# Background turns one projection unit later in the dense stages of a two-layer decoder trunk

## The chip, the cores and the metric

The kernel runs on one core of a Trainium2 chip. Its time is device microseconds (us) from launch to end, the median of several executions; 1670.02 us before (three executions, 1669.08 to 1671.56). All times below are in us unless marked ns.

## The reference

256 tokens of width 2048 go through two layers. Layer 0 is a projection into twelve groups of 512 columns (retention q, k, v, gate, and two halves of a convolution branch), retention over two chunks of 128 for four heads, beside it a gated 31-tap convolution with a layer norm, and an output projection. Layer 1 is a sparse attention: a projection to 16 query heads, 4 key and value heads and a small indexer (16 heads of 64, one key of 64, 16 weights), the 64 best keys of each query by the indexer's score, softmax attention over those, an output projection. After each of the two a residual layer norm and a mixture of experts follow: a router picks 2 of 16 experts, each with a gate-and-up projection (2048 to 1024) and a down projection (512 to 2048), and a second residual layer norm.

```python
m = retention_conv_mixer(h, ...) if layer % 2 == 0 else dsa_mixer(h, ...)
h = layer_norm(DEEPNORM_ALPHA * h + m, mix_ln_g[layer], mix_ln_b[layer])
f = grouped_moe(h, router_w, router_b, moe_w_gu[layer], moe_w_down[layer])
h = layer_norm(DEEPNORM_ALPHA * h + f, ffn_ln_g[layer], ffn_ln_b[layer])
```

## The kernel before

**Stages.** The program is one stream: dense stage of layer 0 (span 0 to about 395), experts of layer 0 (to about 857), dense stage of layer 1 (to about 1195), experts of layer 1 (to the end). Weights come in chunks of 1 MB through SyncE's DMA queue into pages of on-chip memory. At most `ringmax` chunks are held: 4 or 5 in the dense stages, 11 from the point `close_act` on, 20 and then fewer in the experts. A chunk is requested as soon as a page is free.

**Units.** A dense stage is cut into units. A unit is 256 rows of one 512-column weight group: ScalarE copies the piece to a rounded high part, VectorE or GpSimd subtracts for the low part (`split`, L243 and L246, the two engines by turns), and TensorE does 12 matmuls (`mm`, L284 to L286). Eight units make a group. The split of a unit is issued three units ahead of its matmuls. In layer 0 units 0 to 95 are the input projection and 96 to 127 the output projection; the output projection begins with the convolution half of its operand, so units 96 to 99 use that and the retention half is first used by unit 100. In layer 1 units 0 to 15 are the indexer's queries (two groups), 16 to 19 its key and weights (`kiwi_done`, one narrow group), 20 to 27 k, 28 to 35 v, 36 to 67 the four groups q0 to q3 of four heads each, and from 68 on the output projection.

**Order.** Each engine works through its own queue in the order in which the program issues. For unit u the order is: splits of unit u+3, matmuls of u, then, if u is the last of its group, the group's `done` (for q, k and the indexer a rotation: 8 VectorE operations on the accumulator, L703 to L706, and 4 GpSimd additions, L707 and L708), then the hooks of u, and then one step of background work (`bg(1.3)`).

**Background tasks.** Smaller work is written as generators in a queue of tasks. `yield c` with c above 0 charges c to the budget of 1.3 of this step; `yield -1` puts the task aside until the step behind the next unit. So every `yield -1` moves all that follows in that task one unit on. The tasks that the change touches are:

- `conv_ln` of layer 0: normalizes the convolution (`cn`, L548, on VectorE), waits, transposes it on TensorE (`psd`, L556), applies Silu on ScalarE and splits it. Retention heads are other tasks in the same queue.
- `ret_T` of layer 0, a hook: turns a quarter of the gated retention (`sgt`, made at `start_out`, L653) on TensorE (`psr`, L663), and splits it for the output projection. The last one is followed by `close_act`, which opens the ring to 11.
- `kiwi_done.task` of layer 1: turns the indexer's key and weights (`pki`), rotates them, turns the key again (`pki2`, which the trace shows as `pki` L1284), and goes on to the index scores and the top-64 mask.
- `turn` of layer 1: waits, then turns a rotated group on TensorE (`psq`, L1297). It is called once for each of the two indexer query groups, for k, and for each of the four q groups. For a q group the task goes on behind the turn to its four heads, each in four steps that follow one unit after the other: score (`psl` on TensorE, the scaled maximum `amx` with its negation L1395 on VectorE, the exponent L1397 on ScalarE), scaling (reciprocal L1399 and two scalings of `p`, L1401, on VectorE), transposition (`psp`, L1405, TensorE, and a copy to `pT`), output (`pso`, L1411 to L1413, and a copy to `oT`). Heads start one unit apart.

In front of unit 68 `start_out` runs tasks without a budget until 12 heads are finished, and then splits those heads' output for the output projection (`ohi` on ScalarE L1423, `olo` on VectorE L1424):

```python
def start_out():
    while held["heads"] < 12:
        self.bg(1e9)
    self.drop(4)
    oo["hi"], oo["lo"] = self.halves("ohi"), self.halves("olo")
    halves(range(0, 12, 2))
```

Of the kernel before, what the change touches and what calls it, by code (L numbers as in the profile page):

```python
# [80 lines left out]
class Trunk:  # L81
# [376 lines left out]
    def even(self):  # L458
# [6 lines left out]
        def xprep(kp):  # L465
            def f():
                ps = self.psum("psx").rearrange("p (k n) -> p k n", k=2)
                for j in range(2):
                    for t in range(2):
                        c = (2 * kp + j) * P  # L470
                        nc.tensor.transpose(ps[:, j, t * P:(t + 1) * P], self.acc[t][:, c:c + P], self.ident)
                s = slice(2 * kp % 8, 2 * kp % 8 + 2)
                hi, lo = xhi[kp // 4][:, s, :], xlo[kp // 4][:, s, :]
                nc.scalar.activation(hi, ps, AF.Copy)
                nc.vector.tensor_tensor(lo, ps, hi.bitcast(F32), ALU.subtract)
            return f
# [23 lines left out]
        def conv(j, u):  # L500
            if j == 0:
                pg["up"], pg["cy"] = self.page("up", [P, 8, S]), self.page("cy", [P, 8, S])
            up, cy = pg["up"], pg["cy"]
            yield -1
            yield -1
            for b2 in range(2):
                ps = self.psum("psu").rearrange("p (k n) -> p k n", k=2)
                for b in range(2):
                    for t in range(2):
                        c = (b2 * 2 + b) * P  # L510
                        nc.tensor.transpose(ps[:, b, t * P:(t + 1) * P], u[:, t, c:c + P], self.ident)
                c = j * 4 + b2 * 2
                nc.scalar.activation(up[:, c:c + 2, :], ps, AF.Copy)
            yield -1
            for c0 in (j * 4, j * 4 + 2):
                ps = self.psum("pcv").rearrange("p (c n) -> p c n", c=2)
                for i in range(TAPS):
                    for c in (c0, c0 + 1):
                        y, w = ps[:, c - c0, i:], self.cw[:, c, TAPS - 1 - i:TAPS - i]
                        if i:  # L520
                            nc.vector.scalar_tensor_tensor(y, up[:, c, 0:S - i], w, y, op0=ALU.mult, op1=ALU.add)  # L521
                        else:
                            nc.vector.tensor_scalar(y, up[:, c, :], w, self.cvec[:, c:c + 1], op0=ALU.mult, op1=ALU.add)
                        yield 0.33
                nc.scalar.activation(cy[:, c0:c0 + 2, :], ps, AF.Copy)
            if j == 1:
                yield from conv_ln()

        def conv_ln():
            cy = pg["cy"]  # L530
            cn = self.page("cn", [P, 2, 1024])
            self.drop()
            st = ap.tile([P, 2, 2, 6], F32, name="cst6")
            mv = ap.tile([P, 2, 2], F32, name="cmv")
            rs = ap.tile([P, 2], F32, name="crs")
            for t in range(2):
                for h in range(2):
                    ps = self.psum("psc")
                    for b in range(4):
                        nc.tensor.transpose(ps[:, b * P:(b + 1) * P], cy[:, h * 4 + b, t * P:(t + 1) * P], self.ident)  # L540
                    nc.vector.bn_stats(st[:, t, h, :], ps)
                    nc.scalar.activation(cn[:, t, h * 512:(h + 1) * 512], ps, AF.Copy)
                    yield 0.6
                nc.vector.bn_aggr(mv[:, t, :], st[:, t].rearrange("p a b -> p (a b)"))
            self.rstd(rs, mv[:, :, 1])
            yield -1
            for t in range(2):
                nc.vector.tensor_scalar(cn[:, t, :], cn[:, t, :], mv[:, t, 0:1], rs[:, t:t + 1], op0=ALU.subtract, op1=ALU.mult)  # L548
                yield 0.6
            yield -1  # L550
            for kp in range(4):
                ps = self.psum("psd").rearrange("p (k n) -> p k n", k=2)
                for b in range(2):
                    for t in range(2):
                        c = (kp * 2 + b) * P
                        nc.tensor.transpose(ps[:, b, t * P:(t + 1) * P], cn[:, t, c:c + P], self.ident)  # L556
                for b in range(2):
                    c = kp * 2 + b
                    nc.scalar.activation(cy[:, c, :], ps[:, b, :], AF.Silu, bias=self.cvec[:, 16 + c:17 + c], scale=self.cvec[:, 8 + c:9 + c])
                yield 0.3  # L560
            self.drop()
            hi, lo = cc["c"] = [self.page(f"cc{n}c", [P, 8, S], F32R) for n in ("hi", "lo")]
            for c in range(0, 8, 2):
                nc.scalar.activation(hi[:, c:c + 2, :], cy[:, c:c + 2, :], AF.Copy)
                nc.vector.tensor_tensor(lo[:, c:c + 2, :], cy[:, c:c + 2, :], hi[:, c:c + 2, :].bitcast(F32), ALU.subtract)
                yield 0.6
            self.drop()
# [88 lines left out]
        def ret_T(j, b2):  # L656
            def f():
                sg = held["g", j]
                ps = self.psum("psr").rearrange("p (k n) -> p k n", k=2)
                for b in range(2):  # L660
                    for t in range(2):
                        c = (b2 * 2 + b) * P
                        nc.tensor.transpose(ps[:, b, t * P:(t + 1) * P], sg[:, t, c:c + P], self.ident)  # L663
                k = j * 4 + b2 * 2
                hi, lo = cc["hi"][0][:, k:k + 2, :], cc["lo"][0][:, k:k + 2, :]
                nc.scalar.activation(hi, ps, AF.Copy)
                nc.vector.tensor_tensor(lo, ps, hi.bitcast(F32), ALU.subtract)
            return f
# [6 lines left out]
        n = 12 * 8  # L675

        def close_act():
# [2 lines left out]
            self.tasks.append(self.router(0))  # L680
            self.rings(11)
            self.table(AF.Sigmoid)
        hooks = {("pre", n): [start_out], n + 0: [ret_T(0, 0)], n + 1: [ret_T(0, 1)], n + 2: [ret_T(1, 0)],
                 n + 3: [ret_T(1, 1), close_act], ("pre", 0): [xprep(0)], ("split", 0): [xprep(1), lambda: self.warm(3)], ("pre", 1): [xprep(2), xprep(3)]}
        for i in range(2, 6):
            hooks["pre", i] = [xprep(i + 2)]
        self.dense(self.units(gin) + self.units(gout, self.eorder), self.moe_begin, hooks)
# [521 lines left out]
    def odd(self):  # L1209
# [57 lines left out]
        def kiwi_done(ac):  # L1267
            kw = kw80
            nc.scalar.activation(kw, ac[0][:80, 0:S], AF.Copy)

            def task():
                yield -1
                ps = self.psum("pki").rearrange("p (t n) -> p t n", t=4)
                for t in range(2):
                    nc.tensor.transpose(ps[:, t, 0:80], kw[:, t * P:(t + 1) * P], self.ident[:80, :80])
                for t in range(2):
                    self.rope(k2[:, t, 0, :], ps[:, t, 0:64], icos[:, t, :], isin[:, t, :], 1, 32)
                V.tensor_scalar(wi, ps[:, 0:2, 64:80], 1.0 / 32.0, None, op0=ALU.mult)
                nc.gpsimd.tensor_copy(k2[:, :, 1, :], k2[:, :, 0, :])
                yield 1.0  # L1280
                yield -1
                ps = self.psum("pki2")
                for t in range(2):
                    nc.tensor.transpose(ps[:, t * P:(t + 1) * P], k2[:, t].rearrange("p a b -> p (a b)"), self.ident)  # L1284
                nc.scalar.activation(kiT, ps[:, 0:S], AF.Copy)
                yield from index()
            self.tasks.append(task())

        def turn(r, dst, c0):
            yield -1  # L1290
            yield -1
            for b2 in range(2):
                ps = self.psum("psq").rearrange("p (k n) -> p k n", k=2)
                for b in range(2):
                    for t in range(2):
                        c = (b2 * 2 + b) * P
                        nc.tensor.transpose(ps[:, b, t * P:(t + 1) * P], r[:, t, c:c + P], self.ident)  # L1297
                nc.scalar.activation(dst[:, c0 + b2 * 2:c0 + b2 * 2 + 2, :], ps, AF.Copy)
# [43 lines left out]
        def k_done(ac):  # L1342
            r = t4("kr")
            for t in range(2):
                self.rope(r[:, t, :], ac[t], cos[:, t, :], sin[:, t, :], 4, 64)
            self.tasks.appendleft(turn(r, kT(), 0))
# [102 lines left out]
        n = 4 + 8 * 8  # L1449
        hooks = {("pre", n): [start_out], ("pre", n + 12): [last_heads, close_act]}  # L1450
# [103 lines left out]
```

## Time and profile before

| what | us |
|---|---|
| median of three executions | 1670.02 |
| profiled execution | 1669.06 |
| its span, first to last instruction | 1667.3 |
| TensorE busy, summed over the execution | 1629.0 |
| mean granted TensorE clock, share of full | 0.992 |

TensorE is drawn busy for all but some 38 us of the span. Ends of matmuls are modelled in the trace, so a matmul is drawn longer than the distance to the next one; a stall is read from the distance between two starts. The window view gives, per stretch, the busy time of each engine, the granted clock of TensorE and the busy share of the DMA engines.

### The profile page before, as it was taken

The page shows a single profiled execution, that of the slowest core. Times are in us where ns is not written, and L with a number is a line of the kernel's source. Part 1 is how long each engine was busy: PE and PEld are TensorE (multiplying, and loading weights), DVE is VectorE, ACT ScalarE, POOL GpSimd, SP SyncE. Part 2 cuts the span into 40 slices and gives each one's busy share as a digit, 9 for nine tenths or more (in the row PEclk, how much of TensorE's full clock was granted, in tenths as well). Part 3 has the DMA queues.
Part 4 walks back from the last instruction along what each step waited for, and adds up shares of the span by engine and source line. Part 5 has one row for each costly group of instructions (what it writes and reads, how often), then busy time and mean ns, then how long its engine had stood idle before and what let it go on. Part 6 is the DMA issues. An engine that isn't in the chain of part 4 may idle for free. (4 is left out here: it accounts for less than half of the span.)

```text
span 1667.3 us, 21366 instructions
## 1 busy us (share of the span) xinstructions
PE 1629.0 (98%) x8449; PEld 1019.7 (61%) x8449; DVE 783.9 (47%) x1467; ACT 529.0 (32%) x852; POOL 361.4 (22%) x247
## 2 busy tenths in 40 slices
PE   9999999998999999999999999999899999999998
PEld 7888887786435443544357788878635444454534
DVE  5699987633133232335245585664313222322624
ACT  5334345433211211121135444554312221212112
POOL 2446564541000000010004544344200000001001
PEclk9999999998999999999999999999899999999999
DMA  9755544858999999999984454347799999999995
GB/s 352 218 179 182 171 158 166 322 205 317 384 407 419 427 426 426 427 426 426 424 313 152 154 176 139 138 166 272 322 367 414 425 427 427 426 426 427 427 425 195
DMA packets 123164, 528.47 MB, mean 317 GB/s; under 512 B 10650, under 2 KB 11170, under 8 KB 74802
## 3 DMA queue, kind: packets, MB, share of 16 engines
q1 hardware_dynamic: 122130, 525.32, 80.1%
q0 software_dynamic: 784, 1.66, 0.3%
q8 instruction: 69, 1.13, 0.3%
q14 instruction: 37, 0.30, 0.0%
q10 hardware_dynamic: 144, 0.07, 0.0%
HBM read 524.91 MB, written 2.10 MB: 316 GB/s over the span
## 5 line engine op out<-in xcount | busy, mean ns | idle before, releaser
L961 PE MATMUL pgu<-w,X 128*64 128x512 f32 x2048 | 450.9, 593 | 0.9 <-DMA w<-in_moe_w_gu_dram 0.7
L246 POOL TENSOR_TENSOR sp<-w,sp 128x1024 fp32r<-128x1024 f32 (+1 forms) x105 | 265.0, 2532 | 286.6 <-ACT sp L243 272.1
L961 PEld LDWEIGHTS pgu<-w,X 128*64 128x64 f32 x2048 | 144.6, 137 | 286.5 <-issue 269.8
L243 ACT ACTIVATE sp<-w 128x1024 fp32r<-128x1024 f32 (+1 forms) x224 | 226.1, 1045 | 103.8 <-PE acc L286 42.7
L246 DVE TENSOR_TENSOR sp<-w,sp 128x1024 fp32r<-128x1024 f32 (+1 forms) x119 | 180.1, 1519 | 139.3 <-ACT sp L243 138.7
L1005 PE MATMUL pdn<-w,gT 128*64 128x512 f32 x944 | 209.1, 595 | 0.0
L995 DVE SCALAR_TENSOR_TENSOR Yl<-pdn,gs,Yh 64x512 fp32r<-64x512 f32 (+1 forms) x124 | 90.9, 733 | 228.9 <-ACT Yh L994 215.2
L994 ACT ACTIVATE Yh<-pdn,gs 64x512 fp32r<-64x512 f32 (+1 forms) x124 | 82.9, 669 | 230.3 <-PE pdn L1005 171.4
L284 PE MATMUL acc<-sp,xhi 128*128 128x512 f32 x384 | 152.2, 396 | 0.0
L285 PE MATMUL acc<-sp,xhi 128*128 128x512 f32 x384 | 149.7, 390 | 0.3 <-DVE sp L246 0.3
L286 PE MATMUL acc<-sp,xlo 128*128 128x512 f32 x384 | 149.7, 390 | 0.0
L1005 PEld LDWEIGHTS pdn<-w,gT 128*64 128x64 f32 x944 | 65.3, 137 | 121.6 <-issue 116.6
L873 POOL CAST pb<-pt 128x256 bf16<-128x256 f32 x16 | 7.0, 438 | 601.5 <-DVE pt L872 495.7
L964 ACT ACTIVATE sl<-pgu 128x256 f32<-128x256 f32 x32 | 12.3, 385 | 357.0 <-PE pgu L961 357.0
L965 DVE TENSOR_TENSOR sl<-sl,pgu 128x256 f32<-128x256 f32 x32 | 13.5, 422 | 236.8 <-ACT sl L964 236.8
L521 DVE SCALAR_TENSOR_TENSOR pcv<-up,cw,pcv 128x255 f32<-128x255 f32 (+14 forms) x240 | 113.2, 472 | 7.3
L928 DVE TENSOR_SCALAR X<-psg,vp 128x128 f32<-128x128 f32 x128 | 52.5, 410 | 108.0 <-ACT X L930 108.0
L284 PE MATMUL acc<-sp,hhi 128*128 128x512 f32 x240 | 98.7, 411 | 0.4 <-ACT hhi L1234 0.4
L286 PE MATMUL acc<-sp,hlo 128*128 128x512 f32 x240 | 93.9, 391 | 0.0
L285 PE MATMUL acc<-sp,hhi 128*128 128x512 f32 x240 | 93.6, 390 | 0.0
L930 ACT ACTIVATE X<-psg,vp 128x128 f32<-128x128 f32 x128 | 58.6, 458 | 100.5 <-PE psg L921 69.7
L285 PEld LDWEIGHTS acc<-sp,xhi 128*128 128x128 f32 x384 | 72.2, 188 | 15.3 <-DVE sp L246 1.0
(332 smaller groups left out, 2213.0 us busy)
## 6 DMA issues: line engine op xcount, KB each, us to landing
w<-in_moe_w_gu_dram SPq DMA_DIRECT2D x256, 1024.0 KB, 17.5
w<-in_moe_w_down_dram SPq DMA_DIRECT2D x126, 1024.0 KB, 18.9
w<-in_even_w_in_dram SPq DMA_DIRECT2D x46, 1024.0 KB, 5.2
w<-in_odd_w_in_dram SPq DMA_DIRECT2D x32, 1024.0 KB, 5.2
w<-in_even_w_out_dram SPq DMA_DIRECT2D x16, 1024.0 KB, 7.9
w<-in_odd_w_out_dram SPq DMA_DIRECT2D x16, 1024.0 KB, 5.0
acc<-in_x_dram SPq DMA_DIRECT2D x8, 256.0 KB, 8.3
w<-in_even_w_in_dram SPq DMA_DIRECT2D x4, 512.0 KB, 6.6
```

What stands on the lines that cost most here:

```text
L243: nc.scalar.activation(sp[:, 0], src, AF.Copy)
L246: eng.tensor_tensor(sp[:, 1], src, sp[:, 0].bitcast(F32), ALU.subtract)
L284: nc.tensor.matmul(ac, xh[:, x], wh, start=st, stop=False)
L285: nc.tensor.matmul(ac, xh[:, x], wl, start=False, stop=False)
L286: nc.tensor.matmul(ac, xl[:, x], wh, start=False, stop=en)
L521: nc.vector.scalar_tensor_tensor(y, up[:, c, 0:S - i], w, y, op0=ALU.mult, op1=ALU.add)
L928: V.tensor_scalar(X[i][:, k, :], ps[:, b * P:(b + 1) * P], g, sh, op0=ALU.mult, op1=ALU.add)
L930: nc.scalar.activation(X[i][:, k, :], ps[:, b * P:(b + 1) * P], AF.Identity, bias=sh, scale=g)
L961: nc.tensor.matmul(ps[h * 64:(h + 1) * 64, :], X[i][:, k, j * 64:(j + 1) * 64], wv[:, kk, :, h, :], start=k == 0, stop=k == KT - 1)
L994: nc.scalar.activation(hi, po[r, :], AF.Copy, scale=g)
L995: V.scalar_tensor_tensor(lo, po[r, :], g, hi.bitcast(F32), op0=ALU.mult, op1=ALU.subtract)
L1005: nc.tensor.matmul(po[b][half * 64:(half + 1) * 64, :], gT[:, c, h * 64:(h + 1) * 64], wv[:, half ^ j, 2 * b:2 * b + 2, :], start=kk == 0, ...
```

## The change

Five background tasks get one more `yield -1` ahead of a TensorE transposition: the turn of the normalized convolution in layer 0, both turns of the indexer's key in layer 1, and `turn`, which serves the indexer's queries, k, and the four q groups. The four hooks `ret_T` of layer 0 go from behind units 96 to 99 to behind units 97 to 100, and `close_act` with the last of them. No operation is added or removed.

```diff
@@ conv_ln @@
                 yield 0.6
+            yield -1
             yield -1
             for kp in range(4):
                 ps = self.psum("psd").rearrange("p (k n) -> p k n", k=2)
@@ even @@
-        hooks = {("pre", n): [start_out], n + 0: [ret_T(0, 0)], n + 1: [ret_T(0, 1)], n + 2: [ret_T(1, 0)],
-                 n + 3: [ret_T(1, 1), close_act], ...
+        hooks = {("pre", n): [start_out], n + 1: [ret_T(0, 0)], n + 2: [ret_T(0, 1)], n + 3: [ret_T(1, 0)],
+                 n + 4: [ret_T(1, 1), close_act], ...
@@ kiwi_done.task @@
                 yield -1
+                yield -1
                 ps = self.psum("pki").rearrange("p (t n) -> p t n", t=4)
...
                 yield 1.0
                 yield -1
+                yield -1
                 ps = self.psum("pki2")
@@ turn @@
         def turn(r, dst, c0):
+            yield -1
             yield -1
             yield -1
             for b2 in range(2):
```

## Rows read from the trace of the kernel before

**Rows 1.** The page, busy time, share and instructions of each engine.
```profile
PE 1629.0 (98%) x8449; PEld 1019.7 (61%) x8449; DVE 783.9 (47%) x1467; ACT 529.0 (32%) x852; POOL 361.4 (22%) x247
```
**Rows 2.** The chain that ended last, in order of time (start, us, what).
```profile
1604.98 19.80 DMA w<-in_moe_w_gu_dram
1624.82 1.94 PE pgu L961 x8
```
**Rows 3.** Waits of TensorE (waiter <- releaser: us in total, times, longest).
```profile
PE psd L556 <- DVE cn L548: 2.3, 2, 1.9
PE psr L663 <- DVE sgt L653: 1.8, 1, 1.8
PE pki L1284 <- POOL fixed L1279: 1.3, 1, 1.3
PE psq L1297 <- POOL qir L708: 0.7, 2, 0.4
```
**Rows 4.** TensorE's instructions in order, at the convolution's turn (start, us, instruction).
```profile
274.77 0.39 PE L286 MATMUL acc<-sp,xlo 128*128 128x512 f32 x1
277.04 0.30 PE L556 MATMUL psd<-cst,cn 128*128 128x128 f32 x1 [1.88 <-DVE cn L548]
277.76 1.50 PE L556 MATMUL psd<-cst,cn 128*128 128x128 f32 x12 [0.42 <-DVE cn L548]
```
**Rows 5.** Windows of 20 us: engines' busy us, granted clock, DMA share, GB/s.
```profile
340.00:360.00 20.00, 20.00 (x106) 16.24 (x105) 6.39 (x7) 7.52 (x10) 8.89 (x4) 1.00 0.54 189
...
1080.00:1100.00 20.00, 16.92 (x83) 13.75 (x82) 15.45 (x31) 11.10 (x22) 8.16 (x6) 0.91 0.32 106
...
1200.00:1220.00 20.00, 18.53 (x102) 12.83 (x103) 5.69 (x25) 5.20 (x10) 0.64 (x2) 0.81 0.98 391
```
**Rows 6.** In order: the last retention matmul, and the first gating product.
```profile
293.86 0.59 PE L618 MATMUL psy<-v,at 128*128 128x256 f32 x2
...
299.89 1.74 DVE L653 TENSOR_TENSOR sgt<-sgt,yn 128x1024 f32<-128x1024 f32 x1
```
**Rows 7.** TensorE in order, heads 6 and 7 of group q1.
```profile
1044.40 0.39 PE L1387 MATMUL psl<-kv,qT 128*128 128x128 f32 x2
...
1053.13 0.48 PE L284 MATMUL acc<-sp,hhi 128*128 128x512 f32 x1
...
1055.95 0.38 PE L1411 MATMUL pso<-pT,kv 128*128 128x128 f32 x2
...
1056.86 0.48 PE L284 MATMUL acc<-sp,hhi 128*128 128x512 f32 x1
```
**Rows 8.** VectorE in order, the same heads and the rotation of q2.
```profile
1046.01 2.14 DVE L1395 TENSOR_SCALAR amx<-amx 128x2 f32<-128x2 f32 x1
...
1050.14 1.23 DVE L246 TENSOR_TENSOR sp<-w,sp 128x1024 fp32r<-128x1024 f32 x1 [2.00 <-ACT sp L243]
...
1054.10 0.55 DVE L1401 TENSOR_SCALAR p<-p,asm 128x128 f32<-128x128 f32 x2
...
1058.33 0.41 DVE L703 TENSOR_TENSOR qr<-acc,fixed 128x256 f32<-128x256 f32 x1
...
1060.65 0.41 DVE L706 TENSOR_TENSOR rp<-acc,fixed 128x256 f32<-128x256 f32 x1
```
**Rows 9.** GpSimd in order, the same stretch.
```profile
1045.72 2.40 POOL L246 TENSOR_TENSOR sp<-w,sp 128x1024 fp32r<-128x1024 f32 x1 [6.87 <-ACT sp L243]
...
1061.24 0.74 POOL L708 TENSOR_TENSOR qr<-qr,rp 128x256 f32<-128x256 f32 x1
```
**Rows 10.** TensorE in order, in front of and in unit 68.
```profile
1087.21 0.49 PE L1411 MATMUL pso<-pT,kv 128*128 128x128 f32 x2 [0.64 <-ACT pT L1407]
...
1089.14 0.50 PE L284 MATMUL acc<-sp,ohi 128*128 128x512 f32 x1 [0.99 <-ACT ohi L1423]
...
1091.32 0.70 PE L286 MATMUL acc<-sp,olo 128*128 128x512 f32 x1 [1.45 <-DVE olo L1424]
...
1092.25 0.63 PE L285 MATMUL acc<-sp,ohi 128*128 128x512 f32 x1
```

More of the change, by code (lines that the diff above doesn't have):

```diff
@@ L682, in close_act @@
             self.table(AF.Sigmoid)
-        hooks = {("pre", n): [start_out], n + 0: [ret_T(0, 0)], n + 1: [ret_T(0, 1)], n + 2: [ret_T(1, 0)],
-                 n + 3: [ret_T(1, 1), close_act], ("pre", 0): [xprep(0)], ("split", 0): [xprep(1), lambda: self.warm(3)], ("pre", 1): [xprep(2), xprep(3)]}
+        hooks = {("pre", n): [start_out], n + 1: [ret_T(0, 0)], n + 2: [ret_T(0, 1)], n + 3: [ret_T(1, 0)],
+                 n + 4: [ret_T(1, 1), close_act], ("pre", 0): [xprep(0)], ("split", 0): [xprep(1), lambda: self.warm(3)], ("pre", 1): [xprep(2), xprep(3)]}
         for i in range(2, 6):
```

## The prediction

> **What bounds the kernel now.** I read the page's busy times first: TensorE is drawn busy for 98% of the span [rows 1], so a change of order can only win or lose what TensorE stands still. Then the chain of waits in order of time, at its end: the last expert weights arrive by DMA without a break, and TensorE follows the last landing [rows 2]. The expert stages end on the DMA stream. The windows say what that stream starts from: in the output projection of layer 0 the DMA engines are busy 0.54 of the time, while TensorE is busy all of it [rows 5]; the ring of 11 chunks is full then, and further requests wait for TensorE to free pages. So a microsecond that TensorE wins or loses in a dense stage moves the start of the expert stage, its DMA stream and the end by a microsecond. Last I read TensorE's own waits [rows 3] and the order of instructions around each moved turn.
>
> **What the change removes.** Four of TensorE's waits belong to moved turns: 2.3, 1.8, 1.3 and 0.7 of idle time [rows 3]. Idle time understates a stall, since a matmul is drawn 0.39 long while the next starts 0.23 after it (12 in 2.82 between 1053.13 and 1055.95 [rows 7]); each of the six waits hides 0.16 more. 6.1 + 6 x 0.16 = 7.1. Does each go?
>
> - Convolution's turn: the first transposition starts at 277.04 instead of 275.00, and the next one at 277.76 [rows 4], because VectorE's two `cn` operations are not done. A unit of 2.8 and the score matmuls of a retention head (the next task in the queue, whose turn it then is) now stand in front of it. Both parts of the wait (2.65) go. Behind it the Silu and the split of the convolution come a unit later, but their first user is unit 96, three units behind.
> - Gated retention: the product is ready at 301.63, which is 7.8 behind the start of the last retention matmuls at 293.86 [rows 6]. Two units of 2.8 stood between; three now do, with the matmuls themselves 8.6. The wait goes, with 0.8 to spare. The first quarter then has units 98 and 99 to be split before unit 100 needs it, the last one units 101 and 102. `close_act` requests its chunks a unit later on SyncE's queue, but the ring had long been full (0.54 above), so nothing comes of it.
> - Indexer's key and queries: 1.3 and 0.7 of idle wait for GpSimd. The second turn of the key stands two units later against its first matmuls, with 2.8 more between the two turns; the mask comes two units later, at unit 38 by my count of budgets, where head 0 needs it at 47. These go whole (2.4).
>
> At worst one of them stays (the retention's, 2.0): the gain is 5.1 to 7.1, and I take 7.1.
>
> **What it adds: the q groups.** No wait of TensorE stood at the q turns, so there is nothing to win there, but all four steps of each head move a unit too, while the rotations of the next group stay. Counting yields and budgets through the queue: head 3 had its scaling issued behind unit 50 and its transposition behind 51; now 51 and 52. Unit 51 ends group q1, and its rotation (8 VectorE operations) is issued before the background step. So head 3's scaling, which was ahead of the rotation in VectorE's queue, is now behind it, and TensorE's transposition, one unit later, waits for it with all following units queued behind. The same happens to head 7 (rotation of q2 at unit 59) and head 11 (q3 at unit 67). q3 itself has no rotation behind it.
>
> The price, for head 7, counted from its score matmul. The two engines split by turns, so the split in front of head 7's score, VectorE's before, is now GpSimd's, as it was for head 6. For head 6 the negated maximum was held until GpSimd's split ended (1046.01 + 2.14 = 1048.15 against 1045.72 + 2.40 [rows 8, 9]); exponent and ScalarE's copy followed, and VectorE's split of the unit, which stands ahead of the rotation, began at 1050.14 and let the next in 1.15 later: 6.9 behind the score at 1044.40 [rows 7, 8]. Add 0.7, because head 6's exponent, ahead of it on ScalarE, itself comes that much later when its score has to queue behind a VectorE split. Then the rotation, 1058.33 to 1060.65 and 0.33 more: 2.65. Then the reciprocal (some 0.2, an estimate from its size against that of the scalings) and the scalings 0.55 [rows 8]; and 0.5 because GpSimd's rotation additions last until 1061.98, 0.9 past VectorE's [rows 8, 9], and the scaling, like the maximum, would be held by them. Sum 11.5. TensorE needs from the score to the transposition 0.5, a unit 2.8, an output and a transposition 0.91 (1055.95 to 1056.86 [rows 7]), a unit 2.8 and an output 0.6: 7.7. Stall 3.8.
>
> Bounds: if the rotation starts as soon behind its unit as before (1055.95 to 1058.33, 2.4 [rows 7, 8]) and nothing is held, the scaled head is there at 2.4 + 2.65 + 0.75 = 5.8, TensorE at 0.91 + 2.8 + 0.6 = 4.3: 1.5. If the 0.7 comes twice: 4.5. I take 3.8, for heads 3 and 7: 7.6.
>
> Head 11 stands in front of `start_out`, where no unit covers it. Before, three stalls of 0.64, 0.99 and 1.45 idle, 3.6 with 0.16 each [rows 10], held the chain copy, output, `ohi`, `olo`. Now two rounds run there: output of 10 and transposition of 11, then output of 11. From 11.5 the transposition and its copy take 1.1 (0.33 and the 0.80 stall of before), output to `ohi` 1.9 (1087.21 to 1089.14), `olo` 0.8: 15.3; TensorE's own work from the score on is 6.3 (0.5, a unit, 0.91, two outputs and a transposition 1.5, two matmuls). 9.0 of stall against 3.6: 5.4 more; at the lower bound 3.0, at the upper 6.1.
>
> Cost 13.0 (6.0 to 15.1).
>
> **The clock.** After the stalls in front of unit 68 the granted clock of the 20 us window is 0.91, and two matmuls take 0.93 (1091.32 to 1092.25) instead of 0.46 [rows 5, 10]: half clock, 1.2 GHz, for 0.09 x 20 x 2 = 3.6, which costs half of it. After the router's pause it is 0.81 at 1200 to 1220 [rows 5], 7.6 at half clock in that window alone. The stall of 2.65 at the convolution has no slow matmuls behind it (12 transpositions in 1.50 [rows 4]). Heads 3 and 7 each stall longer than that; I let one of the two be followed by half clock: 1.7. Bounds: none, or both and twice as much in front of unit 68: 5.1. By the Trainium skill (TensorE: Matmul & The Clock Gate, What's actually happening) the slow clock is the default that activity lifts, so that both stalls would be paid for: 1.7 more, an estimate with this case's price.
>
> **Sum.** -7.1 + 13.0 + 1.7 = +7.6 on the profiled execution's 1669.06 (its span is 1667.3, with 1.8 around it) makes 1676.7. The median stands 0.96 above the profiled execution: 1677.6.
>
> **Rivals.**
>
> 1. The stalls are at their lower bounds and no clock falls: -7.1 + 6.0, 1669. For it: the order of splits between the engines changes what is held. Against it: the 2.14 hold recurs in the place that head 7 takes.
> 2. Half clock follows both stalls, and lasts longer in front of unit 68, where the standstill of 9.0 is broken only by short outputs: +5.9 + 5.1, 1681, with the upper bound 1683.
> 3. Not slower but faster: the scalings are no bottleneck. It decides at 0.9: if the rotation starts within 0.9 of its unit's last matmul, rotation 2.65 and scaling 0.75 fit into TensorE's 4.3, heads 3 and 7 cost nothing, head 11 one round of some 3 hidden by earlier slack, and the 7.1 remain: 1663. Against it: before, the rotation began 2.4 behind, with the lighter queue in front of it.
> 4. The dense stages' gain and loss are swallowed by the DMA stream: 1670. Against it: the stream itself waits for pages.
>
> **Chances.** Forecast 0.54, rival 1 0.17, rival 2 0.13, rival 3 0.11, rival 4 0.05. What this kernel's measurement tells from no change is about 0.2%, 3.3: slower than 1673.4 are nearly all of the forecast (0.52), rival 2 and a little of rival 1: 0.68; within it most of rival 1, rival 4 and the rest: 0.20; faster than 1666.7 rival 3 and an edge of rival 1: 0.12. The forecast's own range is 1674 to 1681. The range that leaves out 2 in 10 reaches down into rival 1 and up to rival 2's end: 1668 to 1683.
>
> **What would show it.** Right: TensorE's waits no longer name `psd`, `psr`, `pki` or `qir`; instead `psp` L1405 waits for VectorE's `p`, three times, 3 to 4 each, behind units 52 and 60 and in front of 68, where the first matmul with `olo` starts 9 later than its work asks; the granted clock falls near one of them. The experts of layer 0 begin 4.6 earlier than before, those of layer 1 some 6 to 9 later. Wrong: no wait at L1405, or the rotation ahead of no scaling in VectorE's order; or the retention's wait still there; or a shift of the layer 1 experts that doesn't arrive at the end.

## The result, and the profile after

The changed kernel takes 1684.34 us (median of 4 runs, 1681.67 to 1687.91) against 1670.19 for the kernel before (4 runs, 1669.08 to 1671.56): ratio 1.0080, 95% interval 1.0067 to 1.0092. It is slower, as forecast, but by 14.2 where 7.6 was forecast, and the time lies 1.3 above the upper end of the forecast's range of 1668 to 1683. The profiled execution took 1681.67 with a span of 1679.9, 12.6 more than before; it was the shortest of the four, 2.7 below their median.

The page's busy row, which answers to [rows 1], shows nothing of it: TensorE is busy for 97% instead of 98%.

```profile
PE 1631.9 (97%) x8449; PEld 1021.4 (61%) x8449; DVE 780.8 (46%) x1467; ACT 528.6 (31%) x852; POOL 361.2 (22%) x247
```

TensorE's waits (waiter, releaser: total, times, longest) say where to look. Of the four rows of [rows 3] one is left, with 0.2 instead of 1.8. At the top is a wait that the kernel before doesn't have: the transposition of the attention's probabilities, for VectorE's scaling.

```profile
PE psp L1409 <- DVE p L1405: 13.1, 5, 3.3
...
PE pso L1415 <- ACT pT L1411: 2.6, 2, 2.0
...
PE psr L664 <- DVE sgt L654: 0.2, 1, 0.2
```

Five waits, not the three of the prediction. TensorE in order of time at head 3 (start, us, instruction, idle time before it and its releaser) shows why: the head's two pieces of probabilities are waited for one by one. The first two rows are the same work for the head before, without a stall.

```profile
1019.13 0.39 PE L1417 MATMUL pso<-pT,kv 128*128 128x128 f32 x2
...
1022.43 0.38 PE L1415 MATMUL pso<-pT,kv 128*128 128x128 f32 x2
...
1022.87 0.39 PE L1417 MATMUL pso<-pT,kv 128*128 128x128 f32 x2
1026.30 0.33 PE L1409 MATMUL psp<-cst,p 128*128 128x128 f32 x1 [3.05 <-DVE p L1405]
1028.67 0.69 PE L1409 MATMUL psp<-cst,p 128*128 128x128 f32 x2 [2.04 <-DVE p L1405]
...
1033.02 0.38 PE L1415 MATMUL pso<-pT,kv 128*128 128x128 f32 x2
```

The first wait is 3.2 counted from start to start (0.16 more than its idle time), the second 2.3: 5.5. Head 7 shows the same at 1062.40 and 1064.77, 3.0 and 2.3: 5.2. Its stretch begins and ends here:

```profile
1059.21 0.39 PE L1417 MATMUL pso<-pT,kv 128*128 128x128 f32 x2
...
1069.79 0.38 PE L1415 MATMUL pso<-pT,kv 128*128 128x128 f32 x2
```

VectorE at head 3, which answers to [rows 8], has the last step of the rotation, the reciprocal, and then the pair of scalings at 3.21, where it was 0.55 before.

```profile
1024.89 0.41 DVE L707 TENSOR_TENSOR rp<-acc,fixed 128x256 f32<-128x256 f32 x1
1025.22 0.15 DVE L1403 RECIPROCAL asm<-asm 128x2 f32<-128x2 f32 x1
1025.41 3.21 DVE L1405 TENSOR_SCALAR p<-p,asm 128x128 f32<-128x128 f32 x2
```

GpSimd, which answers to [rows 9], runs an addition of the rotation and right behind it its next weight split:

```profile
1025.44 0.72 POOL L709 TENSOR_TENSOR qr<-qr,rp 128x256 f32<-128x256 f32 x1
1026.12 2.34 POOL L246 TENSOR_TENSOR sp<-w,sp 128x1024 fp32r<-128x1024 f32 x1
```

The two ends agree: 1025.41 + 3.21 = 1028.62 and 1026.12 + 2.34 = 1028.46. The first scaling comes out with the end of the addition (TensorE starts on it at 1026.30), the second with the end of the split (1028.67). The Trainium skill (SBUF — State Buffer, Who interferes with whom) states that a `tensor_scalar` can take a pair of ports that VectorE shares with GpSimd, and that the engine that issues second is then blocked for the whole of the other's instruction. This trace agrees: the split is drawn from 1026.12, the second scaling ends with it, and the pair takes 3.21 against 0.55.

In front of unit 68 TensorE, which answers to [rows 10], has four stalls, and the one for `olo` is gone.

```profile
1094.90 0.49 PE L1415 MATMUL pso<-pT,kv 128*128 128x128 f32 x2 [1.96 <-ACT pT L1411]
...
1099.12 0.95 PE L1409 MATMUL psp<-cst,p 128*128 128x128 f32 x3 [3.28 <-DVE p L1405]
...
1100.71 0.79 PE L1415 MATMUL pso<-pT,kv 128*128 128x128 f32 x2 [0.64 <-ACT pT L1411]
...
1103.35 0.80 PE L284 MATMUL acc<-sp,ohi 128*128 128x512 f32 x1 [0.99 <-ACT ohi L1427]
```

With 0.16 each that is 7.5, against 3.6 before: 3.9 more. VectorE shows two things there. Head 11's pair of scalings takes only 1.10, and TensorE waits once for it: GpSimd has its rotation additions in that stretch, but no weight split behind them. And VectorE stands idle for 4.00 ahead of `olo`, so `olo` no longer comes late; before, the rotation of q3 ran directly in front of it, until 1090.52.

```profile
1098.22 1.10 DVE L1405 TENSOR_SCALAR p<-p,asm 128x128 f32<-128x128 f32 x2
...
1103.32 3.10 DVE L1428 TENSOR_TENSOR olo<-oT,ohi 128x512 fp32r<-128x512 f32 x5 [4.00 <-ACT ohi L1427]
```

The windows (stretch, busy us of PE, PEld, DVE, ACT and POOL, granted clock, DMA share, GB/s) show the clock, before first and then after:

```profile
1020.00:1040.00 20.00, 20.00 (x107) 17.05 (x106) 12.05 (x27) 10.95 (x24) 9.94 (x7) 1.00 0.35 107
1060.00:1080.00 20.00, 20.00 (x106) 17.04 (x105) 11.71 (x28) 9.98 (x23) 9.10 (x6) 1.00 0.46 159
```
```profile
1020.00:1040.00 20.00, 14.91 (x71) 12.31 (x70) 9.22 (x14) 8.16 (x14) 7.45 (x6) 0.91 0.22 64
...
1060.00:1080.00 20.00, 15.71 (x69) 12.88 (x69) 8.32 (x18) 6.25 (x13) 6.94 (x6) 0.83 0.38 127
1080.00:1100.00 20.00, 14.76 (x80) 12.16 (x78) 13.26 (x36) 8.35 (x22) 7.56 (x6) 0.91 0.25 83
1100.00:1120.00 20.00, 18.37 (x82) 15.17 (x82) 8.79 (x21) 11.21 (x23) 4.79 (x2) 0.83 0.31 106
```

From 1020 to 1040, 1060 to 1080 and 1080 to 1120 the granted clock was 0.91, 0.83, 0.91 and 0.83, which makes (0.09 + 0.17 + 0.09 + 0.17) x 20 x 2 = 20.8 at 1.2 GHz. Before, it was 1.00, 1.00, 0.91 [rows 5] and 1.00: 3.6. Half of the difference would be 8.6, but a part of the 20.8 lies where TensorE stands still, and costs nothing there. The price is read from the stretches at the two heads. From the last output in front of the stall to the first output behind the next unit, TensorE takes 10.15 at head 3 (1022.87 to 1033.02) and 10.58 at head 7 (1059.21 to 1069.79), where the same work took 3.30 without a stall (1019.13 to 1022.43). Less the stalls of 5.5 and 5.2, that leaves 1.35 and 2.1 for half clock.

The account. In front of the layer 0 experts the gain shows in the router's first matmul, before and after:

```profile
395.20 0.29 PE L746 MATMUL plg<-cst,part 128*128 128x16 f32 x2
```
```profile
391.20 0.29 PE L747 MATMUL plg<-cst,part 128*128 128x16 f32 x2
```

4.0 earlier. Of this 0.4 isn't the change's: the first matmul of unit 0 starts at 7.63 instead of 8.06 already. The indexer's two waits are gone too, and in unit 45 of layer 1, ahead of the first moved q turn, TensorE is 6.8 earlier (before and after):

```profile
1001.47 0.39 PE L284 MATMUL acc<-sp,hhi 128*128 128x512 f32 x1
```
```profile
994.69 0.39 PE L284 MATMUL acc<-sp,hhi 128*128 128x512 f32 x1
```

The 6.8 are the 0.4 of the start, 3.6 of layer 0's edits, 0.2 that arise in layer 0's experts, and 2.6 at the indexer. The router of layer 1 then starts 12.46 later (before and after):

```profile
1193.59 0.29 PE L746 MATMUL plg<-cst,part 128*128 128x16 f32 x2
```
```profile
1206.05 0.29 PE L747 MATMUL plg<-cst,part 128*128 128x16 f32 x2
```

-6.8 + 5.5 + 5.2 + 3.9 = 7.8; the other 4.6 or so of the 12.46 go to matmuls at half clock, 3.45 as read at heads 3 and 7 and the rest, some 1.2 by balance, in front of unit 68. And the 12.46 reach the end: the span is 12.6 longer.

### The profile page after: what moved, and what is told of

It is laid out like the page before. It is cut to its first block, busy times and chain, and to the rows that moved or that the text cites. A ratio compares the mean times of both kernels' runs of the same rounds, so it can differ in the third digit from the quotient of the medians.

```text
span 1679.9 us, 21365 instructions
## 1 busy us (share of the span) xinstructions
PE 1631.9 (97%) x8449; PEld 1021.4 (61%) x8449; DVE 780.8 (46%) x1467; ACT 528.6 (31%) x852; POOL 361.2 (22%) x247
## 4 chain that ended last, share of the span: by engine, by line
PE 80%; DMA 9%; DVE 7%; ACT 2%; issue 1%; POOL 1%; SPq 0%; ACTq 0%; POOLq 0%; DVEq 0%
PE pgu L962 22%; PE pdn L1006 10%; PE acc L284 10%; PE acc L286 10%; PE acc L285 10%; PE psg L922 7%; DMA w<-in_moe_w_gu_dram 6%; PE psa L1025 3%; DMA w<-in_moe_w_down_dram 2%; DVE pcv L521 1%; DVE sp L246 1%; PE pdn L1093 1%; PE acc L263 1%; ACT sp L243 1%; DVE amx L1399 1%
## 5 line engine op out<-in xcount | busy, mean ns | idle before, releaser
L246 DVE TENSOR_TENSOR sp<-w,sp 128x1024 fp32r<-128x1024 f32 (+1 forms) x119 | 171.7, 1448 | 156.8 <-ACT sp L243 156.7
```

The lines of the kernel that those rows point to most:

```text
L246: eng.tensor_tensor(sp[:, 1], src, sp[:, 0].bitcast(F32), ALU.subtract)
```

## Experiments

Theory A: the moved q turns bring the whole loss, and the other edits only win. A1: they do so by the order in VectorE's queue, the rotation ahead of the scaling. H: the second wait of heads 3 and 7 is GpSimd's weight split, which holds the second scaling. C: what the waits don't add up to is half clock behind the stalls. The rivals stand in the expectations. Each ratio is against the kernel before, timed beside it on the same chip.

**Without the wait in the q turns.** On the changed kernel:

```diff
-        def turn(r, dst, c0):
-            yield -1
+        def turn(r, dst, c0, late=True):
+            if late:
+                yield -1
             yield -1
             yield -1
...
-                    yield from turn(r, qT, 0)
+                    yield from turn(r, qT, 0, False)
```

> The change without its fourth q step: the turns of q0 to q3 keep their two waits, all else stays later. Theory A (the loss lies in the q turns alone: head 3, 7 and 11's scaling behind a rotation on VectorE): all of it goes and the gains stay, 4.2 in layer 0 and 2.4 at the indexer: 1663.6, between 1662 and 1665; TensorE has no wait of psp for p over 0.5. Rival B (the later index scores and mask, or the later retention turns, carry part of the loss): 1667 to 1678.

1662.29 (1661.86 to 1665.82), ratio 0.9958 (0.9945 to 0.9972). No wait of TensorE names `psp` any more, and in front of unit 68 the waits of before stand again:

```profile
PE acc L286 <- DVE olo L1429: 1.5, 1, 1.5
PE acc L284 <- ACT ohi L1428: 1.0, 1, 1.0
```

So the rest of the change is a gain of some 8, and the q turns cost some 22. Theory A holds.

**Only the wait in the q turns.** On the kernel before, the same switch with `late=False` as its default, and `True` for the q groups.

> The kernel before, with only the turns of q0 to q3 one unit later. Theory A: the loss without the gains, 1684.3 + 6.6 = 1691, between 1687 and 1694, with psp waiting for p some 13 in all. Rival B: at most half of the loss, 1670 to 1678.

1692.33 (1689.95 to 1694.47), ratio 1.0132 (1.0115 to 1.0148), 21.8 more. The waits:

```profile
PE psp L1407 <- DVE p L1403: 13.0, 5, 3.3
...
PE psd L556 <- DVE cn L548: 2.3, 2, 1.9
...
PE pki L1284 <- POOL fixed L1279: 1.3, 1, 1.3
```

The five new ones are those of the changed kernel, the old ones of [rows 3] stay. The two parts add up: 21.8 - 8.2 = 13.6, and the whole change costs 14.2.

**The scaling ahead of the rotation.** On the changed kernel the background step of units 51, 59 and 67 is run ahead of the unit's own end; the turns of q1 to q3 drop one wait so that they fall behind the same units as in the change.

```diff
-    def dense(self, us, between, hooks=None, budget=1.3, ahead=3, tail=5):
+    def dense(self, us, between, hooks=None, budget=1.3, ahead=3, tail=5, early=()):
...
+            first = i in early
+            if first:
+                self.bg(budget)
...
-            self.bg(budget)
+            if not first:
+                self.bg(budget)
...
-                    yield from turn(r, qT, 0)
+                    yield from turn(r, qT, 0, j == 0)
...
-        self.dense(us + self.units(gout, self.oorder), self.moe_begin, hooks)
+        self.dense(us + self.units(gout, self.oorder), self.moe_begin, hooks, early=(51, 59, 67))
```

> The changed kernel, with the background step of units 51, 59 and 67 ahead of the rotation instead of behind it; all turns and heads stay in the same units. Theory A1 (the order in VectorE's queue is the cause): psp's waits behind units 52 and 60 go, in front of unit 68 one round more than before remains (2 to 4): 1664 to 1669. Rival A2 (the distance of the head's steps to the unit's end is the cause, as splits and exponents run late anyway): waits of 2 or more stay at heads 3 and 7, 1674 to 1682.

1666.94 (1665.31 to 1668.33), ratio 0.9978 (0.9969 to 0.9987). VectorE scales head 3 and rotates behind it, and no wait names `psp`:

```profile
1024.83 0.55 DVE L1410 TENSOR_SCALAR p<-p,asm 128x128 f32<-128x128 f32 x2
1025.30 0.42 DVE L708 TENSOR_TENSOR qr<-acc,fixed 128x256 f32<-128x256 f32 x1
```
```profile
PE pso L1420 <- ACT pT L1416: 2.6, 2, 2.0
```

That order alone gives back 17 of the 22: A1 holds. The output's wait in front of unit 68 stays, since the extra round of heads stays.

**The edits of layer 0 alone.** The changed kernel with the indexer's and the queries' waits of before.

```diff
             def task():
                 yield -1
-                yield -1
                 ps = self.psum("pki").rearrange("p (t n) -> p t n", t=4)
...
                 yield 1.0
                 yield -1
-                yield -1
                 ps = self.psum("pki2")
...
         def turn(r, dst, c0):
-            yield -1
             yield -1
             yield -1
```

> The changes of layer 0 alone (convolution's turn, retention's turns and the opening of the ring one unit later), layer 1 as before. Theory: the 4.2 by which the experts of layer 0 begin earlier reach the end: 1666.0, between 1665 and 1667. Rival: the later opening of the ring, or an expert stage that ends on its DMA stream, takes it back: 1669 to 1671.

1666.86 (1666.01 to 1668.15), ratio 0.9979 (0.9970 to 0.9988), 3.7 less by the medians for the 3.6 that these edits win in layer 0. So the expert stages don't swallow it. That it arrives one for one is shown to about 1 only: between the two profiled executions the router of layer 0 starts 3.1 earlier, and the span is 2.2 shorter. The indexer's waits stand as before:

```profile
PE pki L1285 <- POOL fixed L1280: 1.3, 1, 1.3
```

**Two weight splits on VectorE.** The splits that held the second scaling, those of units 55 and 63, move from GpSimd to VectorE.

```diff
-        eng = nc.gpsimd if self.nsplit % 2 == 0 and self.pool_split else nc.vector
+        eng = nc.gpsimd if self.nsplit % 2 == 0 and self.pool_split and "vec" not in u else nc.vector
...
+        for n_ in (55, 63):
+            us[n_]["vec"] = True
```

> The changed kernel, with the weight splits of units 55 and 63 on VectorE instead of GpSimd; these two follow the rotation's additions in GpSimd's queue. Theory H (the second scaling of heads 3 and 7 is held until GpSimd's split behind the additions ends): the pair of scalings at L1405 falls from 3.2 to about 1.3, the second of psp's two waits from 2.0 to under 0.4, 3.8 less in all and 1 to 2 less of half clock: 1679, between 1677.5 and 1681. Rival (the additions alone hold it, or scalings are slow there by themselves): the pair stays at 3 and the time at 1683 to 1686.

1679.11 (1676.72 to 1681.18), ratio 1.0047 (1.0033 to 1.0061). At head 3 the pair of scalings takes 1.11, both pieces go to TensorE at once, and the waits are three:

```profile
1027.34 1.11 DVE L1405 TENSOR_SCALAR p<-p,asm 128x128 f32<-128x128 f32 x2
```
```profile
PE psp L1409 <- DVE p L1405: 9.1, 3, 3.3
```

5.2 less than the change, for two waits of 2.3 and less half clock behind them: H holds. Head 11, where no split stood behind the additions, had shown the same in the changed kernel with its 1.10. The 0.56 by which 1.11 exceeds 0.55 is what GpSimd's additions alone cost.

**TensorE kept busy in the stalls.** Twenty matmuls of constants ahead of the transposition of heads 3 and 7.

```diff
+            if h in (3, 7):
+                self.warm(20)
```

> The changed kernel, with 20 extra matmuls of constants ahead of the transpositions of heads 3 and 7, 4.3 at full clock, which is less than the 5.5 that TensorE stands still there. Theory C (half clock after these two stalls costs some 4): it stays at full clock behind units 52 and 60, and the time falls to 1680, between 1678.5 and 1682, although TensorE has more work. Rival (VectorE, not TensorE, sets the pace behind a stall, so that half clock there costs nothing): 1684 to 1686; if the extra matmuls run at half clock, 8.5 each, 1690.

1681.08 (1680.11 to 1681.87), ratio 1.0061 (1.0049 to 1.0074). The pause in useful work is as long as before, 4.48 of constants and 1.00 of idle, but the clock stays up:

```profile
1024.63 0.39 PE L1419 MATMUL pso<-pT,kv 128*128 128x128 f32 x2
1024.85 4.48 PE L377 MATMUL warm<-ones 128*128 128x512 bf16 x20
...
1030.44 0.44 PE L1411 MATMUL psp<-cst,p 128*128 128x128 f32 x2 [1.00 <-DVE p L1405]
...
1033.46 0.38 PE L1417 MATMUL pso<-pT,kv 128*128 128x128 f32 x2
```
```profile
1020.00:1040.00 20.00, 19.00 (x101) 14.39 (x100) 9.64 (x15) 8.71 (x16) 8.28 (x7) 1.00 0.25 75
1060.00:1080.00 20.00, 19.23 (x97) 14.43 (x95) 9.53 (x22) 7.13 (x13) 8.27 (x7) 1.00 0.43 157
```

The stretch of head 3 takes 8.83 (1024.63 to 1033.46) instead of 10.15, that of head 7 8.61 instead of 10.58: 1.3 and 2.0 less, so C holds at the two heads. In front of unit 68 the clock is lower than in the changed kernel (0.85 and 0.81 from 1080 to 1120, against 0.91 and 0.83), so not all of it stays. The executions lie within 1.8 of each other; those of the changed kernel within 6.2. The median is 3.3 less, but the two intervals overlap by 0.0007, so what is left of the gain at the end is not settled.

**Eight heads split early.** On the kernel without the q wait, the heads' split into `ohi` and `olo` is taken from `start_out`, whose stalls of 3.6 were still there, and spread over units 62 to 65.

```diff
+        hooks[61] = [first_half]
+        for n_, k_ in ((62, 0), (63, 2), (64, 4), (65, 6)):
+            hooks[n_] = [early_halves(k_)]
...
-            halves(range(0, 12, 2))
+            halves(range(8, 12, 2))
```

> The change with the q turns as before, and heads 0 to 7 split for the output projection behind units 62 to 65 instead of in front of unit 68. Theory: of the three stalls in front of unit 68 (0.8, 1.15, 1.64) the last two and the half clock behind them (6.8, so 3.4) go, unless the splits hold the scalings of heads 8 to 10: 1657.5, between 1656 and 1660. Rival (VectorE and ScalarE have no room in units 62 to 65, and the stalls move there): 1661 to 1664.

1664.13 (1663.08 to 1664.92), ratio 0.9961 (0.9948 to 0.9973): no gain over its base. The theory's 1656 to 1660 failed, and the rival's stalls are there. The stalls moved: the early splits stand ahead of other heads' work in VectorE's and ScalarE's queues.

```profile
PE psp L1410 <- DVE p L1406: 2.1, 3, 1.6
...
PE psq L1302 <- POOL qr L709: 1.2, 1, 1.2
```

**One pair split early.** The same, but only heads 0 and 1, behind unit 61; and the kernel without the q wait once more.

```diff
+        hooks[61] = [first_pair]
...
-            halves(range(0, 12, 2))
+            halves(range(2, 12, 2))
```

> The change with the q turns as before, and of the split of heads 0 to 11 only the pair that unit 68 needs (heads 0 and 1) behind unit 61. Theory: of the stalls in front of unit 68 the two for ohi and olo (1.15 and 1.64) and the half clock behind them go, and the turn of q3, now earlier against its rotation, waits 1.2 for GpSimd's additions instead, as it did with eight heads split early: 1658.5, between 1656.5 and 1661. Rival (one pair stalls VectorE's later work as eight heads did): 1662 or more.

> The change with the q turns as before, a second time, beside the run with the early pair on one chip: 1662.3, between 1661 and 1664; the standstill in front of unit 68 is that of before (0.8, 1.15, 1.6) with half clock behind it.

1661.42 (1660.57 to 1663.70), ratio 0.9942 (0.9929 to 0.9956); the repeat 1664.60 (1662.19 to 1665.52), ratio 0.9952 (0.9939 to 0.9966). Both lie above their ranges, by 0.4 and 0.6. With the pair split early the waits for `ohi` and `olo` are gone; left there are an output's 0.64 and one for the rotated queries, and the clock is not lowered.

```profile
1081.76 0.49 PE L1416 MATMUL pso<-pT,kv 128*128 128x128 f32 x2 [0.64 <-ACT pT L1412]
...
1086.38 0.88 PE L1302 MATMUL psq<-cst,qr 128*128 128x128 f32 x6 [0.82 <-POOL qr L709]
```
```profile
1080.00:1100.00 20.00, 18.54 (x97) 15.39 (x96) 16.45 (x29) 11.44 (x24) 9.30 (x7) 1.00 0.47 159
```

By its median it is the quickest of all, and it beats the kernel before and the changed one; over its own base the gain is not settled, since the intervals overlap.

## Why the prediction was right and where it failed

- **What bounds the kernel.** Right. Stalls of TensorE in a dense stage reach the end, both ways: 12.6 for 12.46 here, and 3.7 by the medians for 3.6 with the edits of layer 0 alone, this one to about 1. Rival 4, the DMA stream, is out.
- **What is removed.** The edits win 6.2 instead of 7.1 up to the q turns: 3.6 for 4.65 in layer 0 and 2.6 for 2.4 at the indexer. The waits of the convolution, the key and the queries are gone as forecast. The retention's wait was to go with 0.8 to spare; 0.2 of idle stayed, because the product was ready 8.9 behind the last retention matmuls (290.77 to 299.66) instead of the 7.8 of before. Some 0.7 of what layer 0 wins less has no wait to its name and stays open. The kernel without the q wait wins 7.3 and 8.2 in its two measurements; layer 0's edits alone win 3.7, so the rest, 3.6 and 4.5, lies with the indexer's edits. Why it is more than the 2.6 of the trace stays open.
- **What is late next.** Right in mechanism and place: `psp` waits for `p` at heads 3, 7 and 11, the rotation ahead of the scaling. Rival 3 is out: the rotation's place decides, as the scaling ahead of it shows.
- **The price of heads 3 and 7: the step that failed.** The prediction let the pair of scalings be held for 0.5, until the end of GpSimd's rotation additions. That part is measured right, 0.56 with the split moved away. But it did not look at what stands next in GpSimd's queue: the weight split starts right behind the addition and holds the second scaling. The pair takes 3.21, a hold of 2.66, 2.1 more than 0.56. The rest of the chain was taken 0.6 to 0.8 too long (first waits of 3.2 and 3.0 against 3.8). So 10.7 instead of 7.6, above the upper bound of 9.0: that bound lengthened another link and left this one at 0.5. (Two sums of TensorE's own work are 0.1 too high in the prediction, 7.7 for 7.6 and 6.3 for 6.2; put right, the forecast would be 0.3 higher.) The row was at hand: the prediction used the same hold, 2.14 behind a GpSimd split, for the maximum [rows 8, 9].
- **In front of unit 68.** 3.9 instead of 5.4, within its bounds of 3.0 to 6.1. The forecast's form (two rounds, no cover) is there; the `olo` wait of 1.45 went, where the forecast had kept 0.8 for `olo`, a term for which it named no row.
- **The clock.** Some 4.6 instead of 1.7, of which 1.35 and 2.1 are read at heads 3 and 7. The choice "one of the two stalls" failed: both were followed by half clock, as rival 2 had it. Constants that kept TensorE busy in both stalls took 3.3 off the two stretches. The Trainium skill (TensorE: Matmul & The Clock Gate, What's actually happening) states that the slow clock is the default and that activity lifts it. These two stalls agree with that, with 0.91 and 0.83 in their windows; the convolution's stall in the kernel before, with 1.00, doesn't show it.
- **Sum.** -6.8 + 14.6 + 4.6 = 12.4, where the forecast had -7.1 + 13.0 + 1.7 = 7.6. Of the 4.8 missing the hold and its chain are 3.1, the clock 2.9, the gain 0.3, less 1.5 at unit 68. The median lies another 1.7 higher above its profiled execution than the 0.96 taken from before.

Rival 1 is out: no stall was at its lower bound, and the clock fell. Rival 2 was the nearest, 1681 with an upper bound of 1683, at 0.13: right about both stalls being followed by half clock, but without the hold.

## What to carry to other kernels

When background work moves by a step, list for each engine what stands ahead of it in the queue at the new place, and also what the other engine that can block it has queued next, not only what it is running: of two small instructions in a row the first can be held by what runs there, and the second by what stands behind it. Price a stall of TensorE with half clock behind it (1.2 to 2.1 here for each stall or group of stalls), unless a stall of the same length in the same kernel is seen without.

## What the hardware showed unexpectedly

- A pair of small VectorE operations (128x128, 0.55 together) was held for 2.66 by two GpSimd instructions in a row: the second piece did not get in between the addition, drawn until 1026.16, and the split, which starts at 1026.12.
- One and the same stall is not always followed by half clock. The convolution's 2.65 had no slow matmuls behind it in the kernel before [rows 4], where its window has clock 1.00 (first fence). With only the q turns moved, code up to there unchanged, it has 0.91 (second), and from the first matmul of unit 90 to that of unit 93 TensorE takes 14.40 instead of 12.75: the half clock costs 1.65 there.

```profile
270.00:290.00 20.00, 17.70 (x90) 14.71 (x89) 12.98 (x9) 11.71 (x19) 10.90 (x6) 1.00 0.34 116
```
```profile
270.00:290.00 20.00, 17.70 (x82) 14.76 (x81) 12.93 (x9) 11.77 (x19) 10.90 (x6) 0.91 0.36 114
```

- This may be why executions of the changed kernel lie 6.2 apart and those with the stalls filled 1.8; that was not shown.
